# Weight preparation for 7-product units in later, evenly spaced steps, each queued behind urgent evictions

## The chip, the cores and the metric

The kernel runs on one core of a Trainium2 chip. The metric is the device time of one execution in microseconds (us). The engines are TensorE (PE, with the weight load PEld beside it), VectorE (DVE), ScalarE (ACT), GpSimd (POOL) and SyncE (SP), which issues most DMAs. Each engine works through its own queue in order.

## What is computed

One step of a decoder layer on 1024 prompt rows and 8 x 4 sample rows, all in fp32:

```python
def swiglu(x, w1, w3, w2):
    return (jax.nn.silu(x @ w1) * (x @ w3)) @ w2
...
# per layer
#  h = LN1(alpha*x + 0.5*SwiGLU_a(x))
#  z = h @ w_in + b_in
#  A = dilated sliding-window attention, 3 head groups
#  B = chunked causal gMLP spatial gating
#  h = LN2(alpha*h + (sigmoid(gA)*(A@w_oa) + sigmoid(gB)*(B@w_ob)) @ w_out)
#  y = LN3(alpha*h + 0.5*SwiGLU_b(h))
```

The model width is 1024, the hidden width 2816. Prompt and sample rows go through the same weights as 1056 columns, in four chunks of 264. Sample attention also reads stored keys and values (`kv`).

## The kernel before

**Stages**, by the times of the trace: hidden units of the first SwiGLU (w1 and w3) to about 450 us, its w2 to about 660, a norm and gates to about 787, 13 pairs of 128-column blocks of w_in to about 1060, attention and gMLP and their projections to about 1490, the hidden units of the second SwiGLU to about 1880, its w2 to the end.

**A product in fp32.** Each operand is split into a high part, a cast on ACT (`split`, L253), and a low part, a subtraction on DVE (L254). `mm3` (L235 to L242) makes three matmuls of 128x128 by 128x264 of them: high by high, high by low, low by high.

**Units of seven products.** Most matrix products run in the Winograd form of Strassen's scheme: a 2x2 block product takes seven products of blocks, in the order 1, 2, 6, 7, 5, 4, 3. A product is 24 matmuls. It needs sums of weight blocks as operands, and `prep` makes them, once for each unit f: it loads the raw weights `ab` (L376) and `cd` (L377) into the pool R (two buffers), then splits `ab`, makes `s12` (L386, L387) and `s34` (L392, L394) in the pool Q, mostly on POOL, and splits `s12`, `s34` and the second half of `cd` (`dd`). High and low parts lie in the pools W and S. Indices f below FB = 22 are w1/w3 units, and the 13 pairs have indices of their own from 0; indices from 22 on are w2 units.

**Which step runs when.** `prep` is a generator that stops at each `yield`. `begin(f)` makes it and runs its first step, at the start of the unit before. `between`, called after each product, runs one more step of the next unit's preparation, and then `tick` gives turns to the queues of other work (`bg`, `slow`, `mid`), such as sample attention. At a unit's start the rest of its preparation is run out (`ready(f)`, or the loop over `preps.pop(f)` for pairs).

**What sets the order on an engine.** The program is traced in this sequence, and a scheduler then orders each engine's queue by priority. Evictions of products run in `urgent()`, which raises their priority and remembers the last instruction of each engine in `self.fence`. Work in `fenced()` is placed behind that instruction on DVE, ACT and SP (not on POOL). `tick` runs its steps in `fenced()`; before, the preparation steps in `between` are not.

**Evictions.** A unit uses three pairs of PSUM banks: `one` for products 1, 6, 5 and 3, `two` for 2, `three` for 7 and 4. In the pairs (`pair`) products 1, 6, 7 and 3 are written out by ACT (`put`, L1034), 2, 5 and 4 are added by DVE (`add`, L1043). In w1/w3 units (`hidden`) 1, 6 and 7 are copied by ACT, the others combined by DVE. In w2 units DVE adds to the sums (L925), and L555 and L533 of the norm run beside them around 660 us.

**Samples.** `sample_rows` runs as slow work in the nine QKV pairs: after some turns it transposes the sample rows of a pair's two blocks on PE (L1375), copies them on DVE (L1377) and sends them to memory through SP (L1381, L1386). `sample` loads slabs of `kv` (L1406) and multiplies them on DVE (L1421, L1432).

Of the kernel before, what the change touches and what calls it, by code (L numbers as in the profile page):

```python
# [16 lines left out]
ALU = mybir.AluOpType  # L17
# [13 lines left out]
FB = 2816 // P  # L31
# [28 lines left out]
REST = 3  # L60
GAP = 4
AFTER = 100
LATE = 16
MID = 3
HOP = (4, 1, 4)
# [18 lines left out]
class Trunk:  # L84
# [285 lines left out]
    def prep(self, src, f, H, engine):  # L370

        nc = self.nc
        lo, hi, n = slice(0, H), slice(H, 2 * H), 2 * H
        with self.tc.high_priority(offset=URGENT):
            ab, cd = self.R([P, D])[:, :n], self.R([P, D])[:, :n]
            nc.sync.dma_start(ab, src[1])  # L376
            dma = nc.sync.dma_start(cd, src[0])  # L377
        self.copy_state(dma, 2)
        tt = engine.tensor_tensor
        ah, al = self.W([P, D]), self.W([P, D])  # L380
        self.split(ah[:, :n], al[:, :n], ab)
        if f == LASTW2:
            h34, l34 = self.held([P, D], F32R), self.held([P, D], F32R)
        yield
        s12 = self.Q([P, D])
        tt(s12[:, lo], cd[:, lo], cd[:, hi], op=ALU.add)  # L386
        tt(s12[:, hi], s12[:, lo], ab[:, lo], op=ALU.subtract)  # L387
        yield
        s34 = self.Q([P, D])
        h12, l12 = self.W([P, D]), self.W([P, D])  # L390
        self.split(h12[:, :n], l12[:, :n], s12[:, :n])
        tt(s34[:, lo], ab[:, lo], cd[:, lo], op=ALU.subtract)  # L392
        yield
        tt(s34[:, hi], ab[:, hi], s12[:, hi], op=ALU.subtract)  # L394
        part = lambda h, l, o=0: [((h, l), o + k * P) for k in range(H // P)]
        if n == D:
            dd = self.S([P, D], F32R)
            self.split(dd[:, lo], dd[:, hi], cd[:, hi])
            p4 = part(dd[:, lo], dd[:, hi])
        else:  # L400
            p4 = []
            for h, l, w in ((ah, al, D - n), (h12, l12, H - (D - n))):
                o = H + len(p4) * P
                self.split(h[:, n : n + w], l[:, n : n + w], cd[:, o : o + w])
                p4 += part(h, l, n)[: w // P]
        yield
        if f != LASTW2:
            h34, l34 = self.S([P, D], F32R), self.S([P, D], F32R)
        self.split(h34[:, :n], l34[:, :n], s34[:, :n])
        self.L[f] = {  # L410
            1: part(ah, al), 2: part(ah, al, H), 5: part(h12, l12), 6: part(h12, l12, H),
            7: part(h34, l34), 3: part(h34, l34, H), 4: p4,
        }
        yield

    def product(self, t, p, f, first):
        while any(p not in t for t in self.T):
# [257 lines left out]
    def ffn(self, w13, w2p, w2, i, mode, resid):  # L675
        nc, preps = self.nc, {}
        plain = PLAIN[: 1 if i == 0 else 2]
        blocks = [f for f in range(FB) if f not in plain] + [FB + g for g in range(NG * (KB // 2))]
        after = dict(zip(blocks, blocks[1:]))
# [53 lines left out]
                begin(after[f])  # L733

        def between(f, bg, slow=0):
            if after.get(f) in preps:
                next(preps[after[f]], None)
            self.tick(bg, slow)

        def load(n):  # L740
# [84 lines left out]
    def out(self, w2, i, mode, ready, between, load):  # L825
# [101 lines left out]
        for c in range(NC):  # L927
            early = 6 if c == 0 else 0
            if mode != "out":
                self.hold_normed(c)  # L930
                if c == 2:
                    self.early = [self.unit(self.a["wzp"][n], slot=True, ahead=AFTER) for n in range(CHUNKED)]
            for n in range(KB):
# [153 lines left out]
    def widen(self):  # L1087
# [13 lines left out]
        preps = {}  # L1101
# [15 lines left out]
        for n in range(CHUNKED, NLEAD):  # L1117
            w = self.unit(a["wzp"][n])
            if n == NLEAD - 1:
                begin(0)  # L1120
            for c in (1, 3, 0, 2):
                self.gate8(w, DENSE[n], c, AF.Sigmoid, STEPS["lead"], 1)
                if n == NLEAD - 1:
                    next(preps[0], None)
        self.A = None
        for f in range(NZ):
            for _ in preps.pop(f):
                pass
            if f < NZ - 1:
                begin(f + 1)  # L1130

            def between():
                if f + 1 in preps:
                    next(preps[f + 1], None)
                self.tick(STEPS["strassen"], 1)

            self.pair(f, between)
            del self.L[f]
# [230 lines left out]

    def sample_rows(self, *blocks):  # L1370
        nc, a = self.nc, self.a
        yield from self.pause(4)
        p = self.ax_tile()[:NS, : 2 * P].rearrange("p (s x) -> p s x", s=2)
        for x, (_, t) in enumerate(blocks):
            nc.tensor.transpose(p[:, x], t[:, NP:], self.ident)  # L1375
        st = self.M([NS, 2, P])
        nc.vector.tensor_copy(st, p)  # L1377
        for x, (nb, _) in enumerate(blocks):
            s, g, hp = nb // 6, (nb % 6) // 2, nb % 2
            L = GROUPS[g][0]  # L1380
            nc.sync.dma_start(  # L1381
                self.sD[g, s, 2 * hp : 2 * hp + 2].rearrange("h t e -> t h e"),
                st[:, x].rearrange("t (h e) -> t h e", h=2),
            )
            if s:
                nc.sync.dma_start(a[f"ws{g}"][:, L - 4 :, 256 * (s - 1) + P * hp : 256 * (s - 1) + P * hp + P], st[:, x])  # L1386
# [522 lines left out]
```

## Time and profile before

| what | us |
|---|---|
| time, median of 3 runs | 2153.39 |
| lowest and highest run | 2152.51, 2158.67 |
| the profiled execution's own time | 2154.51 |
| span of that execution | 2152.5 |
| mean granted PE clock | 0.994 |
| ACT idle for POOL's s12 (W L253 <- Q L387), 14 times | 88.1 |
| DVE idle for kv (M L1432 <- M<-kv), 17 times | 18.4 |

The span runs from the first to the last instruction of the execution that the hardware profiler recorded. Idle time of an engine counts for the end only where another engine that sets the pace waits behind it. A row of a timeline gives the start in us from the span's start, the duration, the engine, the line, what is written and read, and in brackets the idle time before and what ended it. In names, W, S, Q, R, M and X are pools in SBUF, mm and ax PSUM banks, kv, hD, zD and sD tensors in memory.

### The profile page before, as it was taken

The numbers are of one execution on the slowest core, as the hardware profiler recorded it, in microseconds if no ns is written. First come the engines' busy times: TensorE is split into PE (matmuls) and PEld (weight loads), VectorE is DVE, ScalarE is ACT, GpSimd is POOL, SyncE is SP. The second block draws the span as 40 slices with busy tenths as digits, with TensorE's granted clock in tenths as the row PEclk, the third lists the DMA queues.
The fourth block names the chain that finished last, engine by engine and source line by source line (L and its number), as shares of the span: only waits on it lengthen the run. The fifth ranks groups of instructions, "written<-read, shape, count | busy, mean of one in ns | idle before, by whom it ended". The sixth has DMA issues, their size and how long they took to land.

```text
span 2152.5 us, 43254 instructions
## 1 busy us (share of the span) xinstructions
PE 2122.6 (99%) x17307; PEld 2085.6 (97%) x17307; DVE 1549.5 (72%) x2727; ACT 889.4 (41%) x1680; POOL 317.1 (15%) x249
## 2 busy tenths in 40 slices
PE   9999999999999999999999999999999999999997
PEld 8999999999999999999988889999999999999997
DVE  8877767747789834777767758787667777657887
ACT  5444444422124634333476544164444444421224
POOL 0432322200000011323000000000323323100000
PEclk9999999999999999999999999999999999999998
DMA  4444555598885335676865765423454554596852
GB/s 155 145 140 170 183 166 168 189 338 315 327 325 176 130 103 177 201 231 198 296 211 187 223 190 177 154 110 110 144 174 156 183 173 153 194 408 267 311 186 81
DMA packets 168377, 426.51 MB, mean 198 GB/s; under 512 B 24352, under 2 KB 59792, under 8 KB 165488
## 3 DMA queue, kind: packets, MB, share of 16 engines
q1 hardware_dynamic: 167744, 423.21, 56.4%
q8 instruction: 135, 2.21, 0.4%
q10 hardware_dynamic: 432, 0.54, 0.1%
q14 instruction: 66, 0.54, 0.1%
HBM read 304.31 MB, written 165.57 MB: 218 GB/s over the span
## 4 chain that ended last, share of the span: by engine, by line
PE 89%; DVE 4%; DMA 4%; POOL 1%; issue 1%; ACT 0%; SPq 0%; ACTq 0%; DVEq 0%; POOLq 0%
PE ax L242 46%; PE mm L242 39%; DMA R<-wz 1%; PE ax L1206 1%; DMA M<-kv 1%; DMA S<-cD 1%; PE ax L1255 1%; PE ax L1232 1%; DVE W L254 1%; DMA S<-hD 0%; DVE S L632 0%; POOL Q L392 0%; POOL Q L387 0%; DVE S L254 0%; PE ax L621 0%
## 5 line engine op out<-in xcount | busy, mean ns | idle before, releaser
L242 PE MATMUL mm<-S,W 128*128 128x264 f32 x5400 | 713.6, 287 | 8.0 <-ACT S L253 2.3
L242 PE MATMUL ax<-S,W 128*128 128x264 f32 x5400 | 708.6, 285 | 1.3 <-ACT S L1034 1.1
L242 PEld LDWEIGHTS mm<-S,W 128*128 128x128 f32 x5400 | 677.1, 189 | 21.0 <-issue 7.0
L242 PEld LDWEIGHTS ax<-S,W 128*128 128x128 f32 x5400 | 678.5, 189 | 4.0 <-ACT S L1034 2.4
L242 PE MATMUL ax<-S,S 128*128 128x264 f32 x3240 | 475.9, 284 | 1.0 <-ACT S L1034 0.5
L242 PEld LDWEIGHTS ax<-S,S 128*128 128x128 f32 x3240 | 427.7, 188 | 1.7 <-DVE S L1043 0.9
L242 PE MATMUL mm<-S,S 128*128 128x264 f32 x2280 | 359.4, 286 | 2.6 <-DVE S L925 2.6
L242 PEld LDWEIGHTS mm<-S,S 128*128 128x128 f32 x2280 | 311.0, 189 | 3.9 <-issue 2.9
L253 ACT CAST W<-R 128x256 fp32r<-128x256 f32 (+2 forms) x175 | 130.6, 764 | 307.5 <-PE mm L242 139.9
L386 POOL TENSOR_TENSOR Q<-R 128x512 f32<-128x512 f32 x49 | 68.1, 1390 | 800.8 <-DMA R<-w13a 198.2
L254 DVE TENSOR_TENSOR W<-R,W 128x256 fp32r<-128x256 f32 (+2 forms) x175 | 154.6, 887 | 23.3 <-ACT W L253 21.7
L253 ACT CAST W<-Q 128x1024 fp32r<-128x1024 f32 (+1 forms) x78 | 76.8, 984 | 217.2 <-POOL Q L387 88.1
L820 DVE SCALAR_TENSOR_TENSOR S<-ax,S 128x264 f32<-128x264 f32 x240 | 99.7, 429 | 66.1 <-PE ax L242 65.7
L462 DVE TENSOR_TENSOR S<-ax,M 128x264 f32<-128x264 f32 x82 | 32.6, 433 | 144.7 <-PE ax L242 144.7
L254 DVE TENSOR_TENSOR S<-Q,S 128x1024 fp32r<-128x1024 f32 (+1 forms) x78 | 113.6, 1456 | 5.5 <-ACT S L253 5.4
L110 POOL CAST S<-ones 128x1 fp32r<-128x1 f32 x36 | 12.5, 355 | 675.7 <-PE ax L242 226.0
L254 DVE TENSOR_TENSOR W<-Q,W 128x1024 fp32r<-128x1024 f32 (+1 forms) x78 | 90.6, 1161 | 29.6 <-ACT W L253 29.6
L253 ACT CAST S<-Q 128x1024 fp32r<-128x1024 f32 (+1 forms) x78 | 76.7, 984 | 68.4 <-PE ax L242 49.8
L254 DVE TENSOR_TENSOR S<-S,M 128x528 fp32r<-128x528 f32 x72 | 84.6, 1175 | 2.5 <-ACT M L253 0.7
L253 ACT CAST S<-R 128x512 fp32r<-128x512 f32 (+1 forms) x62 | 42.0, 677 | 98.9 <-DMA sumsA<-S 40.6
L387 POOL TENSOR_TENSOR Q<-Q,R 128x512 f32<-128x512 f32 x49 | 81.0, 1653 | 2.7
L394 POOL TENSOR_TENSOR Q<-R,Q 128x512 f32<-128x512 f32 x49 | 79.7, 1627 | 1.2
(209 smaller groups left out, 2042.5 us busy)
## 6 DMA issues: line engine op xcount, KB each, us to landing
ws<-st SPq DMA_DIRECT2D x144, 256.0 KB
S<-sumsA SPq DMA_DIRECT2D x63, 528.0 KB
S<-sumsB SPq DMA_DIRECT2D x63, 528.0 KB
M<-kv SPq DMA_DIRECT2D x96, 256.0 KB
sumsA<-M SPq DMA_DIRECT2D x90, 264.0 KB
sumsB<-M SPq DMA_DIRECT2D x90, 264.0 KB
R<-w13b SPq DMA_DIRECT2D x44, 512.0 KB
R<-w13a SPq DMA_DIRECT2D x42, 512.0 KB
```

Of the source, the lines that this page charges most:

```text
L110: self.nc.gpsimd.tensor_copy(t[:, 0, :1] if len(shape) == 3 else t[:, :1], self.ones[:, :1])
L242: mm = lambda a, b, s, e: nc.tensor.matmul(o, a[:, cc], b, start=s, stop=e, skip_group_check=True)
L253: a = self.nc.scalar.copy(hi, src)
L254: b = self.nc.vector.tensor_tensor(lo, src, hi.bitcast(F32), op=ALU.subtract)
L386: tt(s12[:, lo], cd[:, lo], cd[:, hi], op=ALU.add)
L387: tt(s12[:, hi], s12[:, lo], ab[:, lo], op=ALU.subtract)
L394: tt(s34[:, hi], ab[:, hi], s12[:, hi], op=ALU.subtract)
L462: go(one, 5, False, lambda x: tt(h[:, x, 1], one[x], p7[:, x], op=ALU.add))
L820: nc.vector.scalar_tensor_tensor(y(x, r, e), bank[x], HALF, y(x, r, e), op0=ALU.mult, op1=ALU.add)
L1206: m = nc.tensor.matmul(pS[h][:, r, :nk], q[e, i * P : (i + 1) * P], k[e, k0 : k0 + nk], start=True, stop=True)
L1232: nc.tensor.transpose(pT[r][:, h, o], s[:, r, h, o], self.ident)
L1255: nc.tensor.matmul(pv[0][e, (i % 4) * P : (i % 4 + 1) * P], V[:, i - (nb - 1) + b, e], sT[:, r, h, b * P : b * P + P], start=b == 0, stop= ...
```

## The change

For w1/w3 units and pairs the steps of `prep` are cut at other places: the first step only loads; the second splits `ab` and makes `s12`; the third makes the first half of `s34`; the fourth splits `s12`, makes the rest of `s34` and splits `dd`; the last splits `s34`. For w2 units the steps stay. A new method `advance` runs a step in `fenced()`, in the w1/w3 stage for all units but the last. The last gate before the pairs runs one step more of the first pair's preparation. `sample_rows` pauses 8 turns and not 4.

```diff
+ROWS = 8
...
         self.copy_state(dma, 2)
         tt = engine.tensor_tensor
+        late = f < FB
+        if late:
+            yield
         ah, al = self.W([P, D]), self.W([P, D])
         self.split(ah[:, :n], al[:, :n], ab)
         if f == LASTW2:
             h34, l34 = self.held([P, D], F32R), self.held([P, D], F32R)
-        yield
+        if not late:
+            yield
         s12 = self.Q([P, D])
         tt(s12[:, lo], cd[:, lo], cd[:, hi], op=ALU.add)
         tt(s12[:, hi], s12[:, lo], ab[:, lo], op=ALU.subtract)
         yield
         s34 = self.Q([P, D])
+        if late:
+            tt(s34[:, lo], ab[:, lo], cd[:, lo], op=ALU.subtract)
+            yield
         h12, l12 = self.W([P, D]), self.W([P, D])
         self.split(h12[:, :n], l12[:, :n], s12[:, :n])
-        tt(s34[:, lo], ab[:, lo], cd[:, lo], op=ALU.subtract)
-        yield
+        if not late:
+            tt(s34[:, lo], ab[:, lo], cd[:, lo], op=ALU.subtract)
+            yield
         tt(s34[:, hi], ab[:, hi], s12[:, hi], op=ALU.subtract)
...
+    def advance(self, gen, fenced=True):
+        if gen is not None:
+            with self.fenced() if fenced else ExitStack():
+                next(gen, None)
...
         def between(f, bg, slow=0):
-            if after.get(f) in preps:
-                next(preps[after[f]], None)
+            self.advance(preps.get(after.get(f)), f < FB - 1)
             self.tick(bg, slow)
...
                 if n == NLEAD - 1:
-                    next(preps[0], None)
+                    for _ in range(2 if c == 2 else 1):
+                        next(preps[0], None)
...
             def between():
-                if f + 1 in preps:
-                    next(preps[f + 1], None)
+                self.advance(preps.get(f + 1))
                 self.tick(STEPS["strassen"], 1)
...
     def sample_rows(self, *blocks):
         nc, a = self.nc, self.a
-        yield from self.pause(4)
+        yield from self.pause(ROWS)
```

What this does to the queues is seen in their order. Line numbers after the change are 1 to 13 higher: L253, L254, L925, L1034 and L1043 become L254, L255, L938, L1047 and L1056. First ACT in an early QKV pair, before: the row S_10195 is an eviction of the previous pair's product 3, S_10449 and S_10450 take this pair's products, and W and S rows without S_10449 or S_10450 are casts of weights.

```order
L253 CAST W_10510<-Q_10477 128x1024
L1034 ACTIVATE S_10195<-ax_10189,qb 128x264
L1034 ACTIVATE S_10195<-ax_10190,qb 128x264
L1034 ACTIVATE S_10449<-ax_10443,cols 128x264
L1034 ACTIVATE S_10449<-ax_10444,cols 128x264
L253 CAST W_10690<-R_10684 128x1024
L1034 ACTIVATE S_10450<-ax_10443,qb 128x66x4
L253 CAST S_10553<-R_10434 128x512
L253 CAST S_10586<-Q_10509 128x1024
L1034 ACTIVATE S_10450<-ax_10444,qb 128x66x4
L1034 ACTIVATE S_10450<-mm_10447,qb 128x66x4
L1034 ACTIVATE S_10450<-ax_10448,qb 128x58x4
```

The same pair after the change, from the second eviction of the previous pair's product 3 (S_10191) on:

```order
L1047 ACTIVATE S_10191<-ax_10186,qb 128x264
L1047 ACTIVATE S_10445<-ax_10439,cols 128x264
L1047 ACTIVATE S_10445<-ax_10440,cols 128x264
L254 CAST W_10473<-R_10433 128x1024
L1047 ACTIVATE S_10446<-ax_10439,qb 128x66x4
L1047 ACTIVATE S_10446<-ax_10440,qb 128x66x4
L254 CAST W_10540<-Q_10477 128x1024
L254 CAST S_10545<-R_10434 128x512
L1047 ACTIVATE S_10446<-mm_10443,qb 128x66x4
L1047 ACTIVATE S_10446<-ax_10444,qb 128x58x4
L1047 ACTIVATE S_10446<-ax_10444,qb 128x32
L254 CAST S_10586<-Q_10509 128x1024
```

The cast of s12 from Q_10477 stood ahead of the previous pair's product 3 evictions; it now stands behind this pair's product 6. The cast of `ab` behind product 1 is now of R_10433 (the next pair's) and not of R_10684 (the one after it), and the cast of s34 from Q_10509 moved behind product 7.

Next DVE in the same pair, before, from the adds of product 2 (S_10449 from mm_10446) to the first add of product 5 (S_10450):

```order
L1043 SCALAR_TENSOR_TENSOR S_10449<-mm_10446,S_10449 128x264
L1421 TENSOR_TENSOR M_10271<-M_10271,X_10226 128x512
L1421 TENSOR_TENSOR M_10272<-M_10272,X_10226 128x512
L1377 COPY M_10518<-ax_10515 32x256
L1421 TENSOR_TENSOR M_10273<-M_10273,X_10226 128x512
L254 TENSOR_TENSOR W_10691<-R_10684,W_10690 128x1024
L1422 TENSOR_REDUCE X_10226<-M_10271 128x8
L1422 TENSOR_REDUCE X_10226<-M_10272 128x8
L1422 TENSOR_REDUCE X_10226<-M_10273 128x8
L254 TENSOR_TENSOR S_10553<-R_10434,S_10553 128x512
L254 TENSOR_TENSOR S_10587<-Q_10509,S_10586 128x1024
L1043 SCALAR_TENSOR_TENSOR S_10450<-ax_10443,S_10450 128x66x4
```

And after, from the same add (S_10445 from mm_10442):

```order
L1056 SCALAR_TENSOR_TENSOR S_10445<-mm_10442,S_10445 128x264
L1434 TENSOR_TENSOR M_10258<-M_10258,X_10226 128x512
L1434 TENSOR_TENSOR M_10259<-M_10259,X_10226 128x512
L1434 TENSOR_TENSOR M_10260<-M_10260,X_10226 128x512
L1435 TENSOR_REDUCE X_10226<-M_10258 128x8
L1435 TENSOR_REDUCE X_10226<-M_10259 128x8
L1435 TENSOR_REDUCE X_10226<-M_10260 128x8
L1390 COPY M_10551<-ax_10548 32x256
L255 TENSOR_TENSOR W_10541<-Q_10477,W_10540 128x1024
L255 TENSOR_TENSOR S_10545<-R_10434,S_10545 128x512
L255 TENSOR_TENSOR S_10587<-Q_10509,S_10586 128x1024
L1056 SCALAR_TENSOR_TENSOR S_10446<-ax_10439,S_10446 128x66x4
```

The low of `ab` (W from R_10684) left this place, the low of s12 (W_10541 from Q_10477) came to it, and the copy of the transposed sample rows went behind the sample multiplies.

Last DVE at the end of the first w2 stage, around 665 us, before. S_7995, S_8283 and S_8290 are lows of weights, the rows that read mm are additions to the sums, the rest belongs to the norm.

```order
L254 TENSOR_TENSOR S_7995<-R_7993,S_7994 128x1024
L533 TENSOR_TENSOR M_7678<-M_7678,S_5582 128x528
L555 TENSOR_TENSOR S_5361<-S_5361,ax_7971 128x528
L555 TENSOR_TENSOR S_5554<-S_5554,ax_7971 128x528 x2
L254 TENSOR_TENSOR S_8283<-R_8281,S_8282 128x1024
L925 SCALAR_TENSOR_TENSOR S_5361<-mm_8000,S_5361 128x264
L545 TENSOR_TENSOR M_7991<-M_7678 128x264
L925 SCALAR_TENSOR_TENSOR S_5554<-mm_8016,S_5554 128x264
L925 SCALAR_TENSOR_TENSOR S_5554<-mm_8032,S_5554 128x264
```

And after:

```order
L569 TENSOR_TENSOR S_5361<-S_5361,ax_7971 128x528 x2
L569 TENSOR_TENSOR S_5554<-S_5554,ax_7971 128x528 x2
L255 TENSOR_TENSOR S_7995<-R_7993,S_7994 128x1024
L938 SCALAR_TENSOR_TENSOR S_5361<-mm_8000,S_5361 128x264
L559 TENSOR_TENSOR M_7991<-M_7678 128x264
L938 SCALAR_TENSOR_TENSOR S_5554<-mm_8016,S_5554 128x264
L255 TENSOR_TENSOR S_8283<-R_8281,S_8282 128x1024
L938 SCALAR_TENSOR_TENSOR S_5554<-mm_8032,S_5554 128x264
```

One split (S_8283) moved from ahead of the addition of mm_8000 to behind that of mm_8016.

## The prediction

> **What bounds the kernel now.** I read the page first, then busy time by windows, then the waits of TensorE (PE), and from the longest of them back along the chain ScalarE (ACT), GpSimd (POOL), DMA.
>
> ```profile
> span 2152.5 us, 43254 instructions
> PE 2122.6 (99%) x17307; PEld 2085.6 (97%) x17307; DVE 1549.5 (72%) x2727; ACT 889.4 (41%) x1680; POOL 317.1 (15%) x249
> ```
>
> PE is busy for 2122.6 of 2152.5 us, and the change removes no matmul. At most the 29.9 us in which PE is idle can be won, and what PE loses at a lower clock. So the question is where the idle time lies. Windows over the stages that the change touches (columns: start and end, length, busy time of PE, PEld, VectorE (DVE), ACT and POOL, granted PE clock, DMA share, GB/s):
>
> ```profile
> 50.00:450.00 400.00, 400.00 (x3285) 400.00 (x3285) 289.25 (x392) 172.11 (x303) 119.87 (x76) 1.00 0.51 168
> 1500.00:1870.00 370.00, 370.00 (x3045) 370.00 (x3044) 262.25 (x354) 159.43 (x280) 111.22 (x72) 1.00 0.49 166
> 871.77:892.45 20.68, 20.68 (x172) 20.66 (x170) 16.78 (x26) 7.33 (x13) 5.73 (x4) 1.00 0.53 180
> 892.45:913.96 21.51, 20.98 (x172) 20.54 (x169) 15.31 (x26) 9.29 (x18) 5.51 (x4) 1.00 0.68 210
> 913.96:937.75 23.79, 21.82 (x171) 20.70 (x171) 19.13 (x39) 9.10 (x23) 6.70 (x4) 1.00 0.64 217
> 937.75:960.76 23.01, 22.78 (x172) 22.26 (x173) 19.39 (x39) 8.61 (x19) 6.31 (x4) 0.93 0.67 218
> 960.76:981.41 20.65, 20.65 (x173) 20.63 (x171) 14.76 (x23) 6.88 (x12) 5.88 (x4) 1.00 0.76 240
> ```
>
> In the two long stretches of w1/w3 units, where most prepared weights are, PE is busy 400.00 of 400.00 and 370.00 of 370.00 us. Nothing can be won there, however the preparation is ordered. The other rows run from one pair's sample transposes to the next pair's. An undisturbed pair takes 20.65 or 20.68 us; three take 21.51, 23.79 and 23.01. Against 20.66 that is 0.85 + 3.13 + 2.35 = **6.3 us**. The chain behind it (start, duration, what ran, in brackets the idle time before and what ended it):
>
> ```profile
> 924.98 0.33 SPq L377 DMA_DIRECT2D R<-wz  x1
> 929.82 1.29 POOL L386 TENSOR_TENSOR Q<-R 128x512 f32<-128x512 f32 x1 [16.74 <-DMA R<-wz]
> 931.08 2.46 POOL L392 TENSOR_TENSOR Q<-R,R 128x512 f32<-128x512 f32 x1
> 933.49 1.74 POOL L387 TENSOR_TENSOR Q<-Q,R 128x512 f32<-128x512 f32 x1
> 935.26 1.05 ACT L253 CAST W<-Q 128x1024 fp32r<-128x1024 f32 x1 [13.15 <-POOL Q L387]
> 936.22 1.47 ACT L1034 ACTIVATE S<-ax,qb 128x256 f32<-128x256 f32 x5
> 937.56 1.39 ACT L1034 ACTIVATE S<-ax,cols 128x256 f32<-128x256 f32 x4
> 937.75 0.40 PE L1375 MATMUL ax<-ident,S 128*32 128x128 f32 x2 [1.21 <-ACT S L1034]
> 938.38 4.98 PE L242 MATMUL ax<-S,W 128*128 128x264 f32 x24 [0.23 <-ACT S L1034]
> ```
>
> ACT works in order. Its cast of s12 stands ahead of the previous pair's product-3 evictions, and waits 13.15 us for POOL, which waits for the cd load. ACT had nothing else ready; the evictions behind the cast were wanted by PE, which stood for 1.21 us and then 0.23. After that 24 matmuls took 4.98 us; an undisturbed pair needs 20.66 / 7 = 2.95 us for a product, so about 2 us went in the half clock (0.93 over this pair). The same cast stands in two more places:
>
> ```profile
> 911.75 1.05 ACT L253 CAST W<-Q 128x1024 fp32r<-128x1024 f32 x1 [4.89 <-POOL Q L387]
> 913.96 0.39 PE L1375 MATMUL ax<-ident,S 128*32 128x128 f32 x2 [0.53 <-ACT S L1034]
> 1000.46 1.05 ACT L253 CAST W<-Q 128x1024 fp32r<-128x1024 f32 x1 [5.55 <-POOL Q L387]
> 1002.68 1.49 PE L242 MATMUL ax<-S,W 128*128 128x264 f32 x10 [0.58 <-ACT S L1034]
> ```
>
> **The change, part by part.** *Casts later in the pairs.* No operation goes or comes; the casts and their lows change places. After it the cast of s12 follows product 6's eviction of the next pair. Count from the transposes of the pair in which the cd load is issued (913.96): product 3 ends five products later, at +14.75, and the cast, next in ACT's queue, could start only at 935.26, or +21.3. Its new place is behind the next pair's product 6, at 20.66 + 2.95 = +23.6, and that product's eviction of about 1.47, so +25.1. POOL keeps its order and had s12 ready at +21.3: 3.8 us of slack where there was a stall. Bounds of this term: all 6.3 us return, or only the wait of the first and second pair in part, say 2. I take 6.3, since the undisturbed pairs hold the same matmuls and PE fills them. The stall at 1002.68 goes by the same reasoning: **0.6 us**.
>
> *Transposes after product 6.* Before, they wait for ACT's evictions at a pair's start (the rows at 913.96 and 937.75). After, the wait left in the program is for DVE's old copy and PE itself. Their copy, the sample stores and the cd load behind them on SP come one product (2.95 us) later than the copy stood, within the 3.8 us. Cost: nothing while that lasts; if it is used up, the first rival.
>
> *Half clock.* Of the 6.3 us about 2 are this. What decides when it comes:
>
> ```profile
> 665.58 4.72 PE L242 MATMUL mm<-S,S 128*128 128x264 f32 x24 [1.90 <-DVE S L925]
> 1282.22 1.71 PE L242 MATMUL mm<-S,W 128*128 128x264 f32 x12 [1.29 <-DVE S L1585]
> 1352.96 3.32 PE L242 MATMUL mm<-S,W 128*128 128x264 f32 x25 [1.35 <-DVE S L1711]
> ```
>
> After gaps of 1.90 and 1.21 us, 24 matmuls took 4.72 and 4.98 us; after gaps of 1.29 and 1.35, 25 took 3.32. So a gap above a microsecond costs 1.6 to 2 us more in some cases, and a gap that goes takes that along. The Trainium skill, page "TensorE: Matmul & The Clock Gate", section "Why this matters for your kernels", says otherwise: no idle gap over some 3 us is to be left, since one idle window drops the clock. By it the half clock in the third pair would have another cause and stay, and the sum would be 2 us smaller. The 1.21-us gap with half speed right behind it speaks against the rule as a limit here.
>
> *The stretch around 665.* This is the scheduler's by-product: the diff names nothing there, but DVE's order is another.
>
> ```profile
> 659.00:683.00 24.00, 21.23 (x156) 20.62 (x155) 23.37 (x39) 11.26 (x21) 0.00 (x0) 0.93 0.50 163
> 663.87 1.22 DVE L254 TENSOR_TENSOR S<-R,S 128x1024 fp32r<-128x1024 f32 x1
> 665.00 0.43 DVE L925 SCALAR_TENSOR_TENSOR S<-mm,S 128x264 f32<-128x264 f32 x1
> 676.19 1.73 PE L242 MATMUL mm<-S,W 128*128 128x264 f32 x12 [0.63 <-DVE S L925]
> ```
>
> DVE is busy 23.37 of 24 us here and sets the pace. Before, a second 1.22-us split stands ahead of the eviction that frees PE at 665.58; after, it stands behind. That eviction then comes about 1.1 us earlier (instructions overlap by 0.1), the gap of 1.90 shrinks to about 0.8, near the 0.5 to 0.6 us gaps behind which no half clock is seen, and some 1.8 us of half clock go. Since DVE has no idle time left, part comes back as waits later in the stretch, as at 676.19. Bounds: nothing, to the whole gap and half clock, 4. I take **1.5**.
>
> *New waits.* In the pairs the cast of s12 and of dd now stand ahead of product 7's eviction on ACT, and the lows of s12, dd and s34 ahead of product 5's adds on DVE. Product 3 needs product 5's bank. From the end of product 7: eviction about 1.4, cast 1.05, low 1.22, adds 1.3 make 5.0, against two products, 5.9. That leaves 0.9 us. In w1/w3 units the same order appears, on engines that are busy 72% (289.25 of 400) and 43% there. Also in the last pair the cast of reloaded sums, behind which PE already stood, moves ahead of one more eviction:
>
> ```profile
> 1054.26 1.37 PE L242 MATMUL ax<-S,S 128*128 128x264 f32 x9 [0.52 <-ACT S L1034]
> ```
>
> Bounds of all these: a gain of 0.5 if that stall goes by chance, to 4 us, about one gap of 2 with its half clock. I take a loss of **1.0**, two gaps like the 0.52.
>
> **Sum:** 6.3 + 0.6 + 1.5 - 1.0 = 7.4 us. The profiled execution took 2154.5 us for its span of 2152.5; less 7.4 is 2147.1. It stands 1.1 above the median of the runs, 2153.4, from which the forecast is **2146.0**. The bound of what a measurement of this kernel can tell, 0.3%, is 6.5 us: faster means under 2146.9, slower over 2159.9.
>
> **The rivals.** *The wait only moves (not faster).* If s12 is later than +25.1, its cast holds product 7's eviction and through s34 product 5's adds. It happens where cd lands 3.8 us later, which sample loads on SP or a late copy could do. Or the gain comes back elsewhere in the DVE-bound stretches. For it: several steps of 1 to 3 us here hang on transfers. Against: the 3.8 us are counted from the latest of the three casts. If half of 6.9 stays, and the stretch at 665 gives nothing, the gain is 3.5 less 1.0: 2151.
>
> *DVE late through the sample work (slower).* DVE's order holds, ahead of the lows, multiplies that wait for loads of kv:
>
> ```profile
> DVE M L1432 <- DMA M<-kv: 18.4, 17, 4.0
> 919.17 0.69 DVE L1432 TENSOR_TENSOR M<-M,X 128x512 f32<-128x512 f32 x1 [2.32 <-DMA M<-kv]
> 927.61 1.65 PE L242 MATMUL ax<-S,S 128*128 128x264 f32 x8 [0.38 <-DVE S L1043]
> ```
>
> It has happened once: after a 2.32-us wait PE stood 0.38 for product 5's adds. With the 0.9 us of slack left, a wait of 4.0 would cost up to 3.1 of idle and 1.6 of half clock, 4.7 a pair. One such pair eats most of the gain over the bound, three make it slower than before by 3 x 4.7 - 7.4 = 6.7: 2160. It decides from three pairs on. Against: only 17 waits with a mean of 1.1 us, and one low of 1.2 us fewer in that place of DVE's queue.
>
> *More than forecast.* The stretch at 665 gives its 4, and nothing new appears: 6.9 + 4 = 10.9, so 2142.5.
>
> *The change does little of what it says.* POOL's order is the same, and only the queue of casts moves. If the stalls were due to the load alone, all would stay: 2153. Against: in ACT's order the casts have left the place that PE waited on.
>
> **How the numbers follow.** Forecast, gain of 5 to 9: 0.50, of which 0.38 lie beyond the bound. The wait moves: 0.27, all within. More: 0.10, faster. Little: 0.05, within. Slower rival: 0.08, over the bound. Together faster 0.48, same 0.44, slower 0.08. The likeliest case alone holds 2144 to 2149. The range, 2141 to 2156, takes in the bounds of the stretch at 665 and one new gap with half clock, and leaves out most of the slower rival and the far end of the gain.
>
> **What would show it.** Right: between 890 and 1005 every pair takes about 20.66 us, the transposes have no idle time before them, and ACT's cast of s12 has none on POOL with PE standing behind it; around 665 PE's first gap is under 1 us and the clock stays at full speed. Wrong: waits of PE on L1047 or L1056 (where L1034 and L1043 stand after the change) of over 1 us in the pairs, idle PE inside 50 to 450 or 1500 to 1870, or new gaps with the clock at 0.93 in a window where it was 1.00.

## The result, and the profile after

The changed kernel takes 2150.94 us (median of 22 runs, 2147.73 to 2155.18), the kernel before 2154.91 (22 runs, 2151.29 to 2158.67) beside it. The ratio is 0.9981, with a 95% interval of 0.9975 to 0.9986: **4 us faster**, where 7.4 were forecast. That is clear of the noise of these runs, but inside the 0.3% (6.5 us) below which the prediction calls two kernels the same. The profiled execution's span fell by 3.8 us, from 2152.5 to 2148.7.

The first two lines of the page after (span, then busy time of each engine, its share and its instructions):

```profile
span 2148.7 us, 42884 instructions
PE 2120.8 (99%) x17307; PEld 2086.1 (97%) x17307; DVE 1524.0 (71%) x2727; ACT 881.0 (41%) x1680; POOL 284.7 (13%) x249
```

The number of matmuls is the same. DVE and POOL are busy 25 and 32 us less, with the same instructions; the last section comes back to this.

In the pairs, the windows from one pair's transposes to the next pair's, which now stand behind product 6 (columns as before):

```profile
896.44:917.06 20.62, 20.62 (x172) 20.60 (x170) 17.51 (x30) 9.99 (x20) 5.92 (x4) 1.00 0.69 227
917.06:937.70 20.64, 20.64 (x173) 20.61 (x170) 20.03 (x40) 9.12 (x23) 5.96 (x4) 1.00 0.72 237
937.70:958.35 20.65, 20.65 (x173) 20.62 (x171) 19.54 (x34) 7.40 (x16) 6.32 (x4) 1.00 0.68 225
958.35:979.00 20.65, 20.65 (x173) 20.62 (x170) 15.67 (x24) 8.78 (x16) 6.47 (x4) 1.00 0.77 242
```

PE is busy in them from end to end, and the clock stays at 1.00. The timeline shows why. POOL, then ACT, in the stretch that was the worst before:

```profile
926.24 1.29 POOL L391 TENSOR_TENSOR Q<-R 128x512 f32<-128x512 f32 x1 [14.10 <-DMA R<-wz]
927.48 1.39 POOL L396 TENSOR_TENSOR Q<-R,R 128x512 f32<-128x512 f32 x1
928.83 1.74 POOL L392 TENSOR_TENSOR Q<-Q,R 128x512 f32<-128x512 f32 x1
```

s12 is ready at 930.57, and its cast is no longer next in ACT's queue. ACT evicts the products, and casts s12 behind product 6 of the next pair:

```profile
937.60 0.85 ACT L1047 ACTIVATE S<-ax,qb 128x264 f32<-128x264 f32 x2 [3.56 <-PE ax L243]
938.34 1.05 ACT L254 CAST W<-Q 128x1024 fp32r<-128x1024 f32 x1
```

At 938.34 the cast starts straight behind the eviction, with no idle time and 7.8 us of slack to POOL. Half of that slack was not foreseen. Product 6 of the pair in which cd is loaded starts at 914.59 before and at 914.16 after; counted from there s12 was ready at +20.6 before and is at +16.4 now. SP issues the load of cd 2.2 us sooner in the pair, it takes 1.0 us less to land, and POOL's operation that took 2.46 us takes 1.39:

```profile
922.40 0.38 SPq L378 DMA_DIRECT2D R<-wz  x1
```

The 13.15 us that ACT stood at this cast before are gone, and with them the stalls of PE.

Elsewhere new gaps stand. PE, from four places of the timeline after (a row counts the matmuls inside the stretch that was asked for, so x8 or x12 need not be a whole group):

```profile
665.12 3.18 PE L243 MATMUL mm<-S,S 128*128 128x264 f32 x24 [0.36 <-DVE S L938]
...
675.25 2.06 PE L243 MATMUL mm<-S,W 128*128 128x264 f32 x12 [2.12 <-DVE S L938]
...
1276.06 1.21 PE L243 MATMUL mm<-S,W 128*128 128x264 f32 x8 [1.87 <-DVE S L1598]
...
2112.27 1.72 PE L243 MATMUL mm<-S,W 128*128 128x264 f32 x12 [1.23 <-DVE S L938]
```

**Where the time went.** Both traces hold 16,344 matmuls of 128x264, so the n-th has the same amount of work ahead of it in both. (By the names of its tiles it is another product in 1,394 places of the changed kernel: PE's own order differs a little too, within the pairs, the w1/w3 units and the w2 stages.) The table gives how much longer (+) or shorter (-) the way between two of them is than in the profile of before, in us; boundaries are times in the trace of before. The other rows are the runs of the next section. One single run of them all, of w13_only, was far slower than the rest (6962 us); its ratio leaves that run out.

```
kernel               to 40  -445  -659  -722  -890  -1060  -1488  -1870   -end |  all
after                -0.0  +0.5  +0.5  +0.4  -0.1   -8.1   +1.0   +0.7   +1.2 | -4.0
after_again          +0.3  +0.5  +0.2  -0.1  -0.1   -8.1   +1.2   +0.7   +1.2 | -4.3
before_again         -0.4   0.0  -0.1  -0.5   0.0    0.0   +0.5    0.0    0.0 | -0.5
pairs_only           +1.2   0.0   0.0   0.0  +0.1   -7.8   +0.8   +0.3   -0.3 | -5.7
pairs_only_again     -0.5   0.0   0.0  -0.3  +0.1   -7.8   -0.5   +0.3   -0.3 | -9.0
w13_only             -0.5  +0.8  +0.2   0.0  -0.1   +2.8   -0.8    0.0   +1.1 | +3.5
fence_first          -1.7  +0.8  +1.3   0.0  -0.1   -8.1   +1.5   +0.7    0.0 | -5.6
rows8_alone          -0.6   0.0   0.0  -0.5  -0.1   +1.3   -1.0   +0.3   -0.2 | -0.8
pairs_unfenced       +0.1   0.0   0.0   0.0  -0.1   -0.7   +3.6   +0.3   -0.2 | +3.0
pairs_fence_oldcut   +0.4   0.0   0.0   0.0  +0.1   -2.5   +1.2   +0.3   -0.3 | -0.9
pairs_rows4          -0.5   0.0  -0.1  -0.4  +0.2   -7.7   +2.6   +0.3   -0.2 | -5.9
early_pool           +0.4   0.0  +0.1  -0.4  +0.7   -7.8   +1.3   +0.3   -0.3 | -5.7
early_c3             -0.2   0.0  +0.3  -2.7  +4.3   -7.9   +0.6   +0.8    0.0 | -5.0
```

The pairs give 8.1 us, more than forecast. Half of it is lost in other stages: the first w1/w3 units (to 445), the two w2 stages (445 to 722, and from 1870), and the stages between 1060 and 1870. (The first stretch, to 40 us, differs by -1.7 to +1.2 us among the executions.)

### The profile page after: what moved, and what is told of

It reads as the page before. It is cut to its first block, busy times and chain, and to the rows that moved or that the text cites. A ratio compares the mean times of both kernels' runs of the same rounds, so it can differ in the third digit from the quotient of the medians.

```text
span 2148.7 us, 42884 instructions
## 1 busy us (share of the span) xinstructions
PE 2120.8 (99%) x17307; PEld 2086.1 (97%) x17307; DVE 1524.0 (71%) x2727; ACT 881.0 (41%) x1680; POOL 284.7 (13%) x249
## 3 DMA queue, kind: packets, MB, share of 16 engines
q8 instruction: 135, 2.21, 0.4%
## 4 chain that ended last, share of the span: by engine, by line
PE 90%; DVE 4%; DMA 4%; ACT 1%; issue 1%; SPq 1%; ACTq 0%; DVEq 0%; POOL 0%
PE ax L243 48%; PE mm L243 37%; PE ax L1219 1%; DMA S<-cD 1%; PE ax L1268 1%; PE ax L1245 1%; DMA M<-kv 1%; DMA S<-zD 1%; DVE S L646 1%; DMA S<-hD 0%; DVE M L1445 0%; PE mm L1564 0%; DMA R<-wout 0%; DVE W L255 0%; DVE S L569 0%
## 5 line engine op out<-in xcount | busy, mean ns | idle before, releaser
L255 DVE TENSOR_TENSOR W<-R,W 128x256 fp32r<-128x256 f32 (+2 forms) x175 | 151.6, 868 | 115.8 <-ACT W L254 114.3
L254 ACT CAST W<-R 128x256 fp32r<-128x256 f32 (+2 forms) x175 | 130.7, 764 | 217.0 <-PE ax L243 65.8
L255 DVE TENSOR_TENSOR W<-Q,W 128x1024 fp32r<-128x1024 f32 (+1 forms) x78 | 88.9, 1140 | 100.2 <-ACT W L254 100.2
L255 DVE TENSOR_TENSOR S<-Q,S 128x1024 fp32r<-128x1024 f32 (+1 forms) x78 | 89.0, 1141 | 44.9 <-ACT S L254 44.7
L254 ACT CAST W<-Q 128x1024 fp32r<-128x1024 f32 (+1 forms) x78 | 77.0, 988 | 101.4 <-DVE Q L392 92.8
L480 ACT ACTIVATE S<-S 128x528 f32<-128x528 f32 x82 | 48.6, 638 | 154.6 <-DVE S L479 154.6
L481 DVE TENSOR_TENSOR S<-S,M 128x264 f32<-128x264 f32 x82 | 89.0, 1112 | 14.5 <-ACT S L480 13.5
L254 ACT CAST S<-Q 128x1024 fp32r<-128x1024 f32 (+1 forms) x78 | 76.9, 986 | 24.3 <-DVE Q L403 14.9
L472 ACT COPY M<-ax 128x264 f32<-128x264 f32 x82 | 28.8, 380 | 139.6 <-issue 88.4
L474 ACT COPY M<-ax 128x264 f32<-128x264 f32 x82 | 30.6, 379 | 128.5 <-PE ax L243 128.4
L392 POOL TENSOR_TENSOR Q<-Q,R 128x512 f32<-128x512 f32 x49 | 72.3, 1476 | 0.1
```

What stands on the lines that cost most here:

```text
L254: a = self.nc.scalar.copy(hi, src)
L255: b = self.nc.vector.tensor_tensor(lo, src, hi.bitcast(F32), op=ALU.subtract)
L472: go(one, 1, True, lambda x: copy(r1[:, x], one[x]))
L474: go(one, 6, False, lambda x: copy(u2[:, x], one[x]))
L480: lambda x: nc.scalar.activation(h[:, x], h[:, x], AF.Silu),
L481: lambda x: tt(h[:, x, 0], h[:, x, 0], r1[:, x], op=ALU.mult),
```

## The experiments

Times are medians with the kernel before beside them on the same chip; ratios have 95% intervals.

**The pairs' part alone.** `prep` gets its cut as an argument, true for the pairs only, and the w1/w3 steps are not queued behind evictions:

```diff
-    def prep(self, src, f, H, engine):
+    def prep(self, src, f, H, engine, late):
...
-        late = f < FB
...
-                preps[f] = self.prep(w13[f], f, KH * P, nc.gpsimd if f > 2 else nc.vector)
+                preps[f] = self.prep(w13[f], f, KH * P, nc.gpsimd if f > 2 else nc.vector, False)
...
-            self.advance(preps.get(after.get(f)), f < FB - 1)
+            self.advance(preps.get(after.get(f)), False)
```

> Late, fenced steps and the pause of 8 only in the pairs; the w1/w3 units are prepared as before the change. Theory (the change has two separate effects, a gain of about 8 us in the pairs and a loss of about 1 to 2 us outside of them, of which the w1/w3 part owns what happens around 665 us): the three stretched pairs take about 20.66 us, the gap of 1.9 us at 665 with its half clock is back as before, and the kernel is 6 to 8 us faster than before, about 2147 to 2149. Rival (whatever is won in the pairs is given back later, since waits for DMA in the following stages move with it): the pairs are clean and the time is still only about 4 us below before, about 2151.

2148.39 us against 2152.95, ratio 0.9975 (0.9965 to 0.9985). The gain in the pairs is there (7.8 us), the gap at 665 too, and no loss stands in the w1/w3 units or behind 1870. Against the kernel before the gain is 4.6 us (5.4 by the ratio), less than the 6 to 8 of the first theory; a second measurement, further down, gives 8.6 (7.8 by the ratio). Beside this run the changed kernel took 2150.71, 2.3 us more.

**The w1/w3 part alone.** The reverse: late and queued for the w1/w3 units (`prep`'s new argument is true for them), the pairs, the pause and the last gate as before.

```diff
-            preps[f] = self.prep(a["wz7"][f], f, KH * P, nc.gpsimd if f else nc.vector)
+            preps[f] = self.prep(a["wz7"][f], f, KH * P, nc.gpsimd if f else nc.vector, False)
...
-                self.advance(preps.get(f + 1))
+                self.advance(preps.get(f + 1), False)
...
-ROWS = 8
+ROWS = 4
```

> Late, fenced steps only for the w1/w3 units; the pairs, the pause of 4 and the last gate as before the change. Theory (two separate effects): the stalls in the pairs stay with their three stretched pairs (21 to 24 us), the first gap around 665 shrinks to about 0.4 us and a gap of about 2 us with half clock comes at 675, and the time is 0 to 2 us above before, 2155 to 2157. Rival (the w1/w3 part gives a share of the gain): 1 us or more below before.

2155.96 against 2152.95, ratio 1.0011 (1.0001 to 1.0020): about 2.4 us slower. PE of this run, around 665, at the pairs' start and in the last w2 stage:

```profile
674.51 1.69 PE L243 MATMUL mm<-S,W 128*128 128x264 f32 x7 [1.80 <-DVE S L937]
...
914.89 0.39 PE L1387 MATMUL ax<-ident,S 128*32 128x128 f32 x2 [0.81 <-ACT S L1046]
937.79 0.40 PE L1387 MATMUL ax<-ident,S 128*32 128x128 f32 x2 [0.74 <-ACT S L1046]
...
2119.73 1.47 PE L243 MATMUL mm<-S,W 128*128 128x264 f32 x10 [1.22 <-DVE S L937]
```

The gap at 674 and the one of 1.22 us at 2119 come with this part, the stalls of the pairs stay without the other. The losses of the changed kernel outside the pairs are there: 0.8 to 445, 0.2 to 659, 1.1 at the end. (2.8 us more to 1060 is mostly one stall of 2.12 us at 1055.91 with half clock behind it, where the cast of reloaded sums waits for a load. The same place cost 0.52 and 1.08 in the two profiles of the kernel before, so this part of the 2.4 us may be chance.)

**The pause of 8 alone.** The kernel before with one number changed:

```diff
     def sample_rows(self, *blocks):
         nc, a = self.nc, self.a
-        yield from self.pause(4)
+        yield from self.pause(8)
```

> The kernel before with the pause of 8 turns ahead of the sample rows' transposes and nothing else. Theory (the cast of s12 ahead of product 3's evictions is the cause): the cast still waits for POOL in the same place, so two to four of the stalls stay, PE then waits at product 6 and not at the transposes; gain 0 to 2 us. Rival (the transposes waiting for ACT are what costs): the stalls at 913.96 and 937.75 go, gain 4 us or more.

2155.69 against 2152.95, ratio 1.0014 (1.0005 to 1.0023). ACT, and the PE row that it releases:

```profile
909.54 1.05 ACT L253 CAST W<-Q 128x1024 fp32r<-128x1024 f32 x1 [11.24 <-POOL Q L387]
```

```profile
914.17 2.00 PE L242 MATMUL ax<-S,W 128*128 128x264 f32 x12 [2.16 <-ACT S L1034]
```

The transposes are away from the pair's start, and PE waits there all the same, now at product 6. So they were the messenger. As forecast the stalls stay; that it is a little slower than before was not expected.

**The changed kernel again.**

> The changed kernel once more, for a second profile. If the wait of 1.9 us at 1276 and its half clock are chance, they differ here by 0.5 us or more and the gap of 2.1 us at 675, which an engine's order sets, stays. If both are the change's, both stay within 0.2 us. Time 4 us below before either way.

2150.71 against 2152.95, ratio 0.9990 (0.9982 to 0.9999). Here the gap at 1274 was 1.04 us without half clock: that one is chance. The gap at 675 stayed (1.79), and the columns to 445, to 1060, to 1870 and to the end are the same to 0.1 us: those come with this kernel and not by chance.

**Which half of the change moves the casts.** Three variants of pairs_only: later steps without the queueing, queueing with the old cut, and the old pause.

```diff
-                self.advance(preps.get(f + 1))
+                self.advance(preps.get(f + 1), False)
```

> The kernel pairs_only with the preparation steps of the pairs not queued behind the evictions: later steps and the pause of 8 stay. In ACT's order the cast of s12 then stands ahead of product 3's evictions, as before the change. Theory (queueing behind the evictions is what moves the casts): the stalls behind this cast are back, two to four gaps of 0.5 us or more between 890 and 1005, and the time is within 2 us of before. Rival (the later steps do it): no such gap, 5 us below before.

2156.72 against 2154.96, ratio 1.0007 (0.9998 to 1.0016). The cast of s12 stands where it was and waits for POOL:

```profile
909.42 1.05 ACT L254 CAST W<-Q 128x1024 fp32r<-128x1024 f32 x1 [9.72 <-POOL Q L391]
```

```profile
914.06 2.12 PE L243 MATMUL ax<-S,W 128*128 128x264 f32 x13 [0.99 <-ACT S L1046]
...
1028.39 1.84 PE L243 MATMUL ax<-S,W 128*128 128x264 f32 x13 [1.06 <-ACT S L1046]
```

With a third of 0.92 us at 927.75, for DVE, and smaller ones, the pairs give 0.7 us and not 7.8: the later cut and the pause by themselves do next to nothing, since without the fence the scheduler leaves the cast of s12 where it stood. (The 3.6 us lost between 1060 and 1488 are a matter of their own, see below.)

```diff
-            preps[f] = self.prep(a["wz7"][f], f, KH * P, nc.gpsimd if f else nc.vector, True)
+            preps[f] = self.prep(a["wz7"][f], f, KH * P, nc.gpsimd if f else nc.vector, False)
```

> The kernel pairs_only with the steps of the pairs cut as before the change, but queued behind the evictions. The cast of s12 then stands behind the next pair's product 1 and ahead of its product 6's evictions, which are due about 26 us after the mark where POOL had s12 at 21. Theory (the queueing is enough): no gap of over 0.3 us between 890 and 1005, the same time as pairs_only within 1.5 us. Rival (both are needed): one to three gaps of 0.5 us or more, 3 us or more above pairs_only.

2151.64 against 2154.96, ratio 0.9986 (0.9977 to 0.9996). The rival holds: the pairs give 2.5 us and not 7.8. The wait for POOL is gone, and two others are there. ACT and the PE row behind it:

```profile
961.79 1.05 ACT L254 CAST W<-R 128x1024 fp32r<-128x1024 f32 x1 [5.93 <-DMA R<-wz]
```

```profile
963.27 1.98 PE L243 MATMUL ax<-S,W 128*128 128x264 f32 x14 [0.97 <-ACT S L1046]
...
992.25 1.97 PE L243 MATMUL ax<-S,S 128*128 128x264 f32 x14 [2.21 <-DVE S L1055]
```

With the old cut the cast of `ab` comes in the first step, one pair early, and the fence holds it ahead of product 6's evictions, where it waits 5.93 us for its load. And at 992 DVE is late for product 5's adds:

```profile
981.67 0.69 DVE L1433 TENSOR_TENSOR M<-M,X 128x512 f32<-128x512 f32 x1 [2.98 <-DMA M<-kv]
983.73 0.69 DVE L1433 TENSOR_TENSOR M<-M,X 128x512 f32<-128x512 f32 x1 [1.37 <-DMA M<-kv]
985.05 0.69 DVE L1433 TENSOR_TENSOR M<-M,X 128x512 f32<-128x512 f32 x1 [0.63 <-DMA M<-kv]
```

Three waits for kv, 5 us in all, and then four lows instead of three ahead of the adds. This is the slower rival of the prediction, in a kernel in which its price is seen: 2.21 us. In the changed kernel one low fewer stands there, and it didn't occur.

```diff
-ROWS = 8
+ROWS = 4
```

> The kernel pairs_only with the sample rows' pause at 4 turns as before the change. Theory (the transposes only showed the wait, they did not make it): no gap of over 0.3 us between 890 and 1005, the same time as pairs_only within 1.5 us. Rival (moving the transposes is part of the gain): they wait for ACT or DVE again, 2 us or more above pairs_only.

2148.24 against 2154.96, ratio 0.9970 (0.9959 to 0.9980). No gap in the pairs, 7.7 us won there. The pause of 8 is not needed.

**The stretch around 665.** Two ways to take DVE work out of it. First the lows of three gate weights go to GpSimd, which does nothing there:

```diff
-            self.split(hi[:, :n], lo[:, :n], raw[:, :n])
+            self.split(hi[:, :n], lo[:, :n], raw[:, :n], self.nc.gpsimd if ahead == AFTER else self.nc.vector)
...
-    def split(self, hi, lo, src):
+    def split(self, hi, lo, src, engine=None):
...
-        b = self.nc.vector.tensor_tensor(lo, src, hi.bitcast(F32), op=ALU.subtract)
+        b = (engine or self.nc.vector).tensor_tensor(lo, src, hi.bitcast(F32), op=ALU.subtract)
```

> The kernel pairs_only with the low parts of the three early gate weights made on GpSimd, which is idle there, and not on VectorE: three instructions of 1.22 us fewer for VectorE between 659 and 683 us. Theory (VectorE's work as a whole sets the pace there, not the place of one split): the way from 659 to 722 us is 2 to 3.7 us shorter than in pairs_only, and the gaps there sum to less than 1.2 us. Rival (the stall comes from the order alone): the way is shorter by under 1 us, another gap takes its place.

2148.66 against 2154.96, ratio 0.9972 (0.9960 to 0.9985), no better than pairs_only. The way is 0.5 us shorter than in pairs_only (0.1 than in its second profile), and three gaps of 0.76, 1.41 and 1.36 us stand in it. POOL's and DVE's rows tell what happened:

```profile
663.40 2.38 POOL L255 TENSOR_TENSOR S<-R,S 128x1024 fp32r<-128x1024 f32 x1 [8.71 <-ACT S L254]
666.43 2.40 POOL L255 TENSOR_TENSOR S<-R,S 128x1024 fp32r<-128x1024 f32 x1 [0.65 <-ACT S L254]
```

```profile
664.71 1.36 DVE L558 TENSOR_TENSOR M<-M 128x264 f32<-128x264 f32 x1
...
666.67 2.73 DVE L546 TENSOR_TENSOR M<-M,S 128x528 f32<-128x528 f32 x1
```

While POOL subtracts, DVE's L558 takes 1.36 us where it takes 0.42 elsewhere, and L546 2.73 where it takes 0.70. Of the 3.7 us that DVE was spared, 3.0 came back so in two instructions alone. The rival is right on the time, but for a reason that neither theory had, so this run does not decide between them.

Second, the same three weights are made a chunk of rows later:

```diff
-                if c == 2:
+                if c == 3:
                     self.early = [self.unit(self.a["wzp"][n], slot=True, ahead=AFTER) for n in range(CHUNKED)]
```

> The kernel pairs_only with the three early gate weights loaded and split one chunk of rows later (12 us), so that their lows leave VectorE's queue between 659 and 683 without going to GpSimd. Theory (VectorE's work as a whole sets the pace in that stretch): its gaps sum to less than 1.2 us, the way from 659 to 722 us is 2 to 3.5 us shorter than in pairs_only, and the time 1.5 to 3.5 us lower. Rival (the additions wait for something else, for the norm's work that stands ahead of them): 1.5 us or more of gaps stay and the time is within 1 us of pairs_only.

2150.04 against 2155.02, ratio 0.9980 (0.9971 to 0.9988). The way from 659 to 722 is 2.7 us shorter than in pairs_only (2.4 than in its second profile), as the theory says; the gaps of 0.77 and 1.23 us that are left are more than it said. The time is not: pairs_only once more, beside it, took 2146.47. For the way from 722 to 890 is 4.2 us longer:

```profile
727.54 1.73 PE L243 MATMUL mm<-S,S 128*128 128x264 f32 x12 [1.97 <-ACT M L1006]
```

ACT came to the gate eviction (L1006) that PE waited for only after this:

```profile
724.66 1.03 ACT L254 CAST W<-R 128x1024 fp32r<-128x1024 f32 x1
725.71 1.28 ACT L1006 ACT_TABLE_LOAD   x1
727.00 0.48 ACT L1006 ACTIVATE M<-mm,cols 128x264 f32<-128x264 f32 x1
```

So DVE's work does set the pace at 665: with 3.7 us of it gone the way is 2.4 to 2.7 us shorter. Putting it off gave the time to another wait.

**Chance.** Two kernels once more:

> The kernel pairs_only once more. If the stretch from 1060 to 1488 us differs between executions by chance of transfers, it differs from the first profile of the same kernel by 0.5 us or more, while the pairs agree within 0.3 us. If it doesn't, what that stretch took longer than before is the change's.

2146.47 against 2155.02, ratio 0.9964 (0.9951 to 0.9977). The pairs agree to 0.1 us with the first profile; the way from 1060 to 1488 differs by 1.3 us.

> The kernel before once more, for a second profile: the same question for the stretches from 1060 to 1488 us, where by chance it would differ from the first by 0.5 us or more, and from 890 to 1005 us, where the three stretched pairs, if they hang on a load's arrival, may differ by 1 us or more.

One time of 2154.95 (span 2152.0). The way from 1060 to 1488 differs by 0.5 us between these two profiles of the kernel before; 890 to 1060 is the same in sum, with 1.46 us of gap at 937 and 0.26 at 913 where the first had 1.21 and 0.53.

**The queueing in the first SwiGLU only.**

```diff
-            self.advance(preps.get(after.get(f)), f < FB - 1)
+            self.advance(preps.get(after.get(f)), i == 0 and f < FB - 1)
```

> The changed kernel with the w1/w3 steps queued behind the evictions in the first SwiGLU only; VectorE's order in the second one is then that of before. Theory (the queueing in the w1/w3 units costs time in both, about 0.5 us in the first units and about 1.2 us in the second w2 stage): the way from 1870 us to the end is 1.2 us or more shorter than in the changed kernel, the 0.5 us of 40 to 445 us stay, and the pairs are clean. Rival (the late pairs delay the end through the loads): that way stays as in the changed kernel within 0.3 us.

2150.02 against 2153.72, ratio 0.9982 (0.9973 to 0.9991). The way from 1870 to the end is 1.2 us shorter than in the changed kernel, exactly what it lost there, and PE's gap at 2112 is 0.47 us again where it was 1.23. The column to 445 keeps its loss (0.8). The one to 659 loses 1.3, with a gap of 0.64 at 648 that stands in no other profile here, so the time as a whole is no better than the changed kernel's.

## Why the prediction was half right

**The pairs: right, and a little more.** The step "the cast moves behind product 6, 3.8 us of slack where there was a stall" held: the cast starts 24.2 us behind product 6 of the pair that loads cd, forecast was 24.5 (+25.1 from its mark), and no pair stalls. That the slack is 7.8 us there and not 3.8 is luck: the prediction had the load of cd come 2.95 us later in the pair and s12 no sooner, and the load came 2.2 us sooner. Forecast 6.9 us, measured 8.1 in two profiles. 0.8 of the 1.2 more is the stall at 1054, for which the forecast had only a bound. The half clock of the third pair went with its gap, as forecast. The transposes cost nothing, as forecast; nor do they gain (pairs_rows4). What the prediction didn't see is which edit does it: the cut (with the pause) alone gives 0.7 us, the queueing 2.5, both 7.8.

**The stretch around 665: wrong.** The step "some 1.8 us of half clock go", with the shorter gap before it, took a waiting or slower PE for lost time, though the same paragraph says that DVE sets the pace. The first gap did shrink, from 1.90 to 0.36, and at 672 the changed kernel was 2.0 us ahead of the kernel before, where it had been 1.1 behind at 660. But a split that changes places takes no work from DVE, which is busy 22.88 and 23.31 of the 24 us from 659 to 683 in the two profiles after. The additions later in its queue came no earlier, and the gap of 2.12 at 675 with its half clock took all of it back; in the second profile gaps of 1.79 and 1.13, without half clock, did. The kernel before shows the same in its own second profile. Its PE rows:

```profile
665.09 3.16 PE L242 MATMUL mm<-S,S 128*128 128x264 f32 x24 [1.90 <-DVE S L925]
...
675.27 1.74 PE L242 MATMUL mm<-S,W 128*128 128x264 f32 x12 [1.75 <-DVE S L925]
```

Here no half clock followed the gap of 1.90 (24 matmuls in 3.16 us, not 4.72), and the next gap was 1.75 and not 0.63. Over the whole stretch the two differ by 0.5 us. Forecast a gain of 1.5; measured between a loss of 0.4 and a gain of 0.1. (Of the rows that the prediction set beside this one, the 25 matmuls in 3.32 us are those behind the gap of 1.35 alone; behind the gap of 1.29 it shows 12 in 1.71.)

**New waits: the right kind, in the wrong place, and too small.** The term of 1.0 us was counted in the pairs, where none came. The w1/w3 units, which the prediction named without an amount of their own, and the w2 stages, which this term left out, lost 0.5 (to 445), 0.2 to 0.5 (to 659) and 1.2 (from 1870). w13_only has all of these without the pairs' part, and in fence_first, without the queueing in the second SwiGLU, the last of them is gone. DVE of the kernel before ahead of its gap of 0.42 us at 2118, then of the changed kernel ahead of the gap at 2112:

```profile
2111.79 0.43 DVE L925 SCALAR_TENSOR_TENSOR S<-mm,S 128x264 f32<-128x264 f32 x1
...
2113.15 2.42 DVE L632 TENSOR_TENSOR S<-S,ax 128x1056 f32<-128x1056 f32 x2 [0.59 <-PE ax L621]
2115.49 2.41 DVE L555 TENSOR_TENSOR S<-S,ax 128x1056 f32<-128x1056 f32 x2
2117.82 1.10 DVE L925 SCALAR_TENSOR_TENSOR S<-mm,S 128x264 f32<-128x264 f32 x3
```

```profile
2107.13 2.41 DVE L646 TENSOR_TENSOR S<-S,ax 128x1056 f32<-128x1056 f32 x2
2109.46 2.41 DVE L569 TENSOR_TENSOR S<-S,ax 128x1056 f32<-128x1056 f32 x2
2111.79 0.43 DVE L938 SCALAR_TENSOR_TENSOR S<-mm,S 128x264 f32<-128x264 f32 x1
```

In both, four norm additions, 4.7 us of work, stand ahead of the addition that PE waits for. After the change one addition fewer to the sums is done before them, so PE comes to wait sooner and longer. That gap makes 0.7 of the 1.2; most of the rest is a gap of 0.43 at 1918.54, for a cast on ACT, which fence_first hasn't either. The queueing was put on w1/w3 steps, but the scheduler's order of what follows them, on PE too, is another.

In the first units PE has no gap at all. The mean distance between starts of matmuls rose from 121.85 to 122.01 ns (60 to 440 us, single instructions of the trace). It did so in all four profiles with the w1/w3 part (after, after_again, w13_only, fence_first) and in none of the others; whether the cut or the queueing does it, and why a matmul takes 0.16 ns longer, stays open. So does the 0.7 between 1488 and 1870, again without a gap: fence_first has it too, without the queueing there, early_c3 has 0.8 without the w1/w3 part, and w13_only has none.

**1060 to 1488: in part a wait for a transfer, the rest not settled.** The changed kernel took 1.0 and 1.2 us longer there in two profiles. pairs_only took 0.8 longer and 0.5 shorter, and all the kernels here range from -1.0 to +3.6. Some of the waits that differ are for transfers (at 1274 DVE waits 3.64 us for cD in the one profile after, 3.08 in the first of before). One wait does go with the clean pairs, for the load of zD. PE, in the changed kernel and in pairs_only:

```profile
1067.29 0.30 PE L1522 MATMUL ax<-ident,S 128*128 128x128 f32 x1 [0.44 <-DMA S<-zD]
```

```profile
1068.59 0.30 PE L1521 MATMUL ax<-ident,S 128*128 128x128 f32 x1 [1.48 <-DMA S<-zD]
```

In the eight profiles without a gap in the pairs it is 0.4 to 2.3 us, in the six others 0 to 0.6: PE comes to this transfer sooner, and some of what the pairs won is waited for there. Over the whole stretch this does not stand out from the spread, and no other wait in it was tied to the change.

Put together: 8.1 from the pairs, less 0.5, 0.3 and 1.2 that come with the w1/w3 part (the last with its queueing; the others were not taken apart), 0.7 between 1488 and 1870 and 1.1 between 1060 and 1488, is 4.3; the profiles' spans say 3.8 and 4.1, the times 4.0. Without the w1/w3 part the kernel is faster than the changed one: ratios of 0.9975 and 0.9964 to before, against 0.9981 and 0.9990.

The rival "the wait only moves" gave 2151, which is what came. Its sum (half of the pairs' gain, less 1.0) is not what happened, so that match is luck; its second condition, that the gain comes back in stretches that DVE paces, is what the w2 stages show.

## What to carry to other kernels

An operation that waits for a slow chain belongs, in an in-order queue, behind the evictions that the bottleneck needs next; here, where a scheduler sets the order, that took a fence as well as a later step. Make such a change only where the trace shows a stall behind it: the same edit in stages without a gap reordered a neighbour and cost 2 us. And in a stretch that another engine paces, a gap or a half clock on TensorE need not be a loss to be won back: count the pacing engine's work over the whole stretch.

## What the hardware showed unexpectedly

**VectorE slows down while GpSimd works on SBUF.** The groups of the low of s34 in the first units (50 to 450 us, 20 instructions of one shape), before and then after:

```profile
L254 DVE TENSOR_TENSOR S<-Q,S 128x1024 fp32r<-128x1024 f32 x20 | 35.5, 1775 | 0.0
```

```profile
L255 DVE TENSOR_TENSOR S<-Q,S 128x1024 fp32r<-128x1024 f32 x20 | 24.5, 1226 | 14.9 <-ACT S L254 14.9
```

The same instruction took 1775 ns on average and then 1226; it is part of the 25 us that DVE was busy less. Before, 16 of the 20 ran beside an operation of POOL, and 12 of them took 1.97 to 2.34 us (the other four 1.22 all the same); after, none did. It was free here, as PE never waited. early_pool shows the price directly. The Trainium skill, page "GPSIMD Engine Reference", section "1. Specifications", says that GpSimd shares its SBUF interfaces with VectorE and names instructions with two SBUF inputs; these rows agree.

**The half clock is not decided by the gap's length.** Gaps of 1.21 and 1.46 us at the third pair were followed by half clock in both profiles of before. The same gap of 1.90 at 665 was followed by it in the first profile of before and in pairs_only, and not in the second profile of before nor in rows8_alone; nor were gaps of 2.21 (pairs_fence_oldcut, 992) and 2.29 (fence_first, 1068). In the clock records it always starts on a grid of 3.413 us: in the first profile of before at 666.57, 939.63 and 2141.13, which are 80 and 352 such steps apart. The gap of 1.90 that was followed by it lay whole in one step, up to 666.57; in rows8_alone a step's end cut it into 1.49 and 0.41. So where a gap falls on that grid bears on it, and differs from execution to execution; it is not the whole rule, since in the second profile of before 1.85 of the 1.90 lay in one step.
